# SSD decay with one additive mask and a per-head Exp on ScalarE, and the gated norm weight folded into w_out

## The chip, the cores and the metric

The kernel runs on one core of a Trainium2 chip. Its engines are TensorE (PE; its weight loads are listed apart as PEld), VectorE (DVE), ScalarE (ACT) and GpSimd (POOL); SyncE (SP) issues nearly all of the DMAs. The metric is the device time of one execution in microseconds (us), as the median of the runs; lower is better. Each engine works through its own instructions in order, and semaphores hold an instruction until what it needs is there.

## The reference, cut to what matters

The model is one step of a decoder trunk with two layers: a Mamba-2 SSD layer, then a latent attention layer (MLA), for a prompt of 1024 tokens and 8 samples of 8 tokens. The change lies wholly in the SSD layer. Its scan works in chunks of 128 tokens, with 32 heads of width 64 in 8 groups of 4 heads, and a state of 128 per head:

```
a = dt * a_head                          # a_head < 0, so a < 0
a_cs = cumsum(a)                         # within the chunk
decay[l, s] = exp(a_cs[l] - a_cs[s])     # for s <= l, else 0
y_diag = ((C B^T) * decay) @ (x * dt)    # per head, C B^T per group
states = B^T @ (x * dt * exp(a_cs[-1] - a_cs))
y_off  = (C @ state before the chunk) * exp(a_cs)
y = (y_diag + y_off + d_skip * x) * silu(z)
y = rms_norm over each group of 256 columns (y) * norm_w
out = y @ w_out
```

`norm_w` has one weight for each of the 2048 columns of y, and these columns are the rows of `w_out`, so `(y * norm_w) @ w_out` and `y @ (norm_w[:, None] * w_out)` are the same sum.

## The kernel before

**Matrix products.** Most of them are made in three passes over a high and a low part of each operand (`split`, lines 127 to 130: ScalarE copies the high part into a rounded type, VectorE or GpSimd subtracts it for the low part). The small products of the scan with the decay (lines 581 to 583) are made in full fp32.

**Stages.** `layer_ssd` (753) normalises x, projects group 0, works out dt and the cumulative sums for all tokens (`ssd_dt`, 335), and then runs over the groups: `ssd_scan` of group g gives a fraction of a step after each of its nine token tiles (eight prompt chunks and the 64 sample tokens), and the projections, convolution and gates of group g + 1 (`Group.steps`, 483) are traced in between. The scan of the last group is interleaved with the first half of the output projection (`ssd_outproj` "a", which needs groups 0 to 3 only: rows 0 to 1023 of `w_out`). The second half ("b") follows, and then the MLA layer.

**One tile of the scan, prompt case** (521 to 672). TensorE transposes x (two blocks) and B into one PSUM bank `trp` (537 to 540). ScalarE copies x out as `xsT` (542) and B as high and low parts. VectorE multiplies x by dt into `xdt` (555), from that PSUM bank. GpSimd multiplies `xsT` by tok slot 2 into `xdd` (558), which is split into `xddh` (ScalarE) and `xddl` (GpSimd); TensorE multiplies these with B into the state update `st` (586). TensorE makes the scores C B^T in the bank `cb`, of which there is one (569), and VectorE multiplies them by a 0/1 mask into `cbm` (571). A DMA on SP's queue copies the four heads' cumulative sums, spread over all partitions, into `M` (573; two buffers). Four VectorE instructions, one for each head, subtract the token's own sum and clip at zero (575); one ScalarE Exp covers all four heads (577); one VectorE product applies `cbm` (578); four matmuls multiply M by `xdt` into the bank `py` (582). Then y is put together by VectorE and GpSimd (656 to 661), ScalarE squares it and sums the squares (662), GpSimd multiplies it by the norm weight `nw` (663), and SP's queue stores it to `y_d` (664). The sample tile does the same with 64 tokens and also updates eight states; its product `pv` (603) uses the `cb` bank as well.

**Output projection.** `load_wout` (695) loads eight blocks of 128 rows of `w_out` for each half into two raw buffers, copies the high part on ScalarE (703) and subtracts the low part on GpSimd for even blocks and on VectorE for odd ones (704). A raw buffer is free for the next load when its low part is made. `ssd_outproj` (708) loads y, scales it by the group norms, transposes and splits it, and accumulates all eight blocks of a half into a bank `pj`, of which there are two (`poa` for the first half, `pob` for the second).

**What sets the order.** In the SSD layer nobody writes the order of an engine's instructions: the framework takes them by priority, which is program order, and places each at the time at which its own timing model thinks it ready. Buffers of a tag are handed out in turn. In the heads and the sample part of the MLA layer the order of TensorE and GpSimd is that of the program.

Of the kernel before, what the change touches and what calls it, by code (L numbers as in the profile page):

```python
# [36 lines left out]
NPG = PAST // PAGE  # L37
SCALE = (NOPE + ROPE) ** -0.5
NEG = -1e30
GB = 4  # L40
NKT = 4
LEAD = 2
# [101 lines left out]
def ssd_tiles(k):  # L144
    cp, nc = k.cs, k.nc
    k.masku = cp.tile([128, 128], F32, name="masku")
    k.masks = cp.tile([64, 128], F32, name="masks")
    k.blkm = cp.tile([64, NB], F32, name="blkm")
    k.yssq = cp.tile([128, 9, G], F32, name="yssq")
    k.tok = cp.tile([128, 9, 4, H], F32, name="tok")  # L150
    k.decp = cp.tile([128, H, 8], F32, name="decp")
    k.decs = cp.tile([128, 16, 8], F32, name="decs")
    k.dtb = cp.tile([128, H], F32, name="dtb")
    k.dsk = cp.tile([128, H], F32, name="dsk")
    k.tok3 = cp.tile([96, 2, H], F32, name="tok3")
    k.blk3 = cp.tile([96, 4], F32, name="blk3")
    k.alog = cp.tile([128, H], F32, name="alog")
    nc.sync.dma_start(k.alog, k.I["ssd_a_log"][0].partition_broadcast(128))
    nc.scalar.activation(k.alog, k.alog, AF.Exp)
    k.convT = cp.tile([128, 32, 24], F32, name="convT")  # L160


def ssd_consts(k):
    nc, I = k.nc, k.I
    nc.sync.dma_start(k.masku, I["c_masku"])
    nc.sync.dma_start(k.masks, I["c_masks"])
    nc.sync.dma_start(k.blkm, I["c_blkm"])
    for j in range(3):
        nc.sync.dma_start(k.blk3[32 * j : 32 * j + 32], I["c_blkm"][:32, :4])
    nc.gpsimd.memset(k.yssq, 1.0)  # L170
    nc.sync.dma_start(k.dtb, I["ssd_dt_bias"][0].partition_broadcast(128))
    nc.sync.dma_start(k.dsk, I["ssd_d"][0].partition_broadcast(128))
# [162 lines left out]
def ssd_dt(k, pool, psum):  # L335
    nc, I = k.nc, k.I
    blks = pool.tile([64, 128], F32, name="blks")
    nc.sync.dma_start(blks, I["c_blks"])
    ones = pool.tile([128, 128], F32, name="ones")
    nc.gpsimd.memset(ones, 1.0)  # L340
    alog = k.alog
    x = k.dtr.rearrange("p i h -> p (i h)")
    n = 9 * H
    u = pool.tile([128, n], F32, name="dtu")
    nc.scalar.activation(u, x, AF.Abs)
    nc.scalar.activation(u, u, AF.Exp, scale=-1.0)
    nc.scalar.activation(u, u, AF.Ln, bias=ones[:, 0:1])
    dt = pool.tile([128, n], F32, name="dt")
    nc.vector.scalar_tensor_tensor(dt, x, 0.0, u, op0=ALU.max, op1=ALU.add)
    a = pool.tile([128, 9, H], F32, name="dta")  # L350
    nc.vector.scalar_tensor_tensor(a, dt.rearrange("p (i h) -> p i h", h=H), -1.0,
                                   alog.unsqueeze(1).to_broadcast([128, 9, H]), op0=ALU.mult, op1=ALU.mult)
    af = a.rearrange("p i h -> p (i h)")
    pa = psum.tile([128, 512], F32, tag="y", name="dpa", bufs=PB["y"])
    pt = psum.tile([128, 512], F32, tag="y", name="dpt", bufs=PB["y"])
    for p, l, ls in ((pa, k.masku, k.masks), (pt, ones, blks)):
        nc.tensor.matmul(p[:, 0:256], l, af[:, 0:256], start=True, stop=True)
        nc.tensor.matmul(p[:, 256:288], ls, af[:64, 256:288], start=True, stop=True)
    acs = pool.tile([128, n], F32, name="acs")
    nc.vector.tensor_copy(acs, pa[:, :n])  # L360

    def tokv(j):
        return k.tok[:, :, j]

    def v(t):
        return t[:, :n].rearrange("p (i h) -> p i h", h=H)

    nc.gpsimd.tensor_copy(tokv(0), v(acs))
    nc.gpsimd.tensor_copy(tokv(1), v(dt))
    nc.vector.tensor_tensor(u, pt[:, :n], acs, op=ALU.subtract)  # L370
    nc.scalar.activation(u, u, AF.Exp)
    nc.vector.tensor_tensor(tokv(2), v(u), v(dt), op=ALU.mult)
    nc.scalar.activation(tokv(3), v(acs), AF.Exp)
    for j in range(3):
        for q in range(2):
            nc.sync.dma_start(k.tok3[32 * j : 32 * j + 32, q], k.tok[32 * q : 32 * q + 32, 8, 2])
    nc.scalar.activation(k.decp, pt[:, :256].rearrange("p (i h) -> p h i", h=H), AF.Exp)
    p = psum.tile([128, 512], F32, tag="tr", name="acsp", bufs=PB["tr"])
    for j in range(2):
        nc.tensor.transpose(p[:, j * 128 : j * 128 + 128], acs[:, j * 128 : j * 128 + 128], k.ident)  # L380
    nc.tensor.transpose(p[:H, 256:320], acs[:64, 256:288], k.ident[:64, :64])
    acsT = pool.tile([128, 320], F32, name="acsT")
    nc.vector.tensor_copy(acsT[:, :256], p[:, :256])
    nc.vector.tensor_copy(acsT[:H, 256:], p[:H, 256:320])
    k.acs_d = k.dram.tile([8, H, 128], F32, name="acs_d")
    k.acss_d = k.dram.tile([H, 64], F32, name="acss_d")
    nc.sync.dma_start(k.acs_d.rearrange("(j i) h t -> (i h) j t", j=2), acsT[:, :256].rearrange("p (j t) -> p j t", j=2))
    nc.sync.dma_start(k.acss_d, acsT[:H, 256:])
    sel = pool.tile([64, 2, 128], F32, name="selp")
    nc.gpsimd.memset(sel, 0.0)  # L390
    nc.gpsimd.memset(sel[:, 0, 0:64], 1.0)
    nc.gpsimd.memset(sel[:, 1, 64:128], 1.0)
    ra = pool.tile([64, 2, 16, NB], F32, name="ra")
    nc.vector.tensor_tensor(ra, a[:64, 8].rearrange("p (c two) -> p two c", two=2).unsqueeze(3)
                            .to_broadcast([64, 2, 16, NB]),
                            bass_bcast2(k.blkm, 2, 16), op=ALU.mult)
    pd = psum.tile([128, 512], F32, tag="tr", name="decp", bufs=PB["tr"])
    mm3(nc, pd[:, :128], [(sel[:, j], ra[:, j].rearrange("p c b -> p (c b)")) for j in range(2)])
    nc.scalar.activation(k.decs, pd[:, :128].rearrange("p (c b) -> p c b", b=NB), AF.Exp)
# [121 lines left out]
def ssd_scan(k, gr, pools):  # L521
# [2 lines left out]
    g = gr.g  # L524
    S = None
    hs = slice(4 * g, 4 * g + 4)
    nw = sp.tile([128, 256], F32, tag="nw", name=f"nw{g}", bufs=1)
    nc.sync.dma_start(nw, I["ssd_norm_w"][0, 256 * g : 256 * g + 256].partition_broadcast(128))
    for i in ORDER[g]:
        t0, m = TILES[i]  # L530
        sl = slice(t0, t0 + m)
# [19 lines left out]
        def v3(t):  # L551
            return t[:m].rearrange("p (h q) -> p h q", q=64)

        xdt = sp.tile([128, 256], F32, tag="xdt", name="xdt" + tag, bufs=2)
        nc.vector.tensor_tensor(v3(xdt), v3(p[:, 0:256]), hb(1), op=ALU.mult)  # L555
        if not smp:
            xdd = sp.tile([128, 256], F32, tag="xdd", name="xdd" + tag, bufs=1)
            nc.gpsimd.tensor_tensor(v3(xdd), v3(xsT), hb(2), op=ALU.mult)
# [8 lines left out]
        nc.gpsimd.tensor_tensor(v3(xD), v3(xsT), k.dsk[:m, hs].unsqueeze(2).to_broadcast([m, 4, 64]), op=ALU.mult)  # L567
        pc = psum.tile([128, 512], F32, tag="cb", name="cb" + tag, bufs=PB["cb"])
        nc.tensor.matmul(pc[:m, :m], B, C, start=True, stop=True)
        cbm = sp.tile([128, 128], F32, tag="cbm", name="cbm" + tag, bufs=1)  # L570
        nc.vector.tensor_tensor(cbm[:m, :m], pc[:m, :m], (k.masks if smp else k.masku)[:m, :m], op=ALU.mult)
        M = sp.tile([128, 4, 128], F32, tag="M", name="M" + tag, bufs=2)
        nc.sync.dma_start(M[:m, :, :m], (k.acss_d[hs] if smp else k.acs_d[i, hs]).partition_broadcast(m))
        for h in range(4):
            nc.vector.tensor_scalar(M[:m, h, :m], M[:m, h, :m], tk[:, 0, 4 * g + h : 4 * g + h + 1], 0.0,  # L575
                                    op0=ALU.subtract, op1=ALU.min)
        nc.scalar.activation(M[:m, :, :m], M[:m, :, :m], AF.Exp)  # L577
        nc.vector.tensor_tensor(M[:m, :, :m], M[:m, :, :m],
                                cbm[:m, :m].unsqueeze(1).to_broadcast([m, 4, m]), op=ALU.mult)
        py = psum.tile([128, 512], F32, tag="y", name="py" + tag, bufs=PB["y"])  # L580
        for h in range(4):
            nc.tensor.matmul(py[:m, h * 64 : h * 64 + 64], M[:m, h, :m], xdt[:m, h * 64 : h * 64 + 64],  # L582
                             start=True, stop=True)
        if not smp:
            ps = psum.tile([128, 512], F32, tag="st", name="st" + tag, bufs=PB["st"])
# [74 lines left out]
            nc.vector.tensor_tensor(y, py[:, :256], xD, op=ALU.add)  # L660
        nc.vector.tensor_tensor(y[:m], y[:m], z, op=ALU.mult)
        nc.scalar.activation(xD[:m], y[:m], AF.Square, accum_out=k.yssq[:m, i, g : g + 1])  # L662
        nc.gpsimd.tensor_tensor(y[:m], y[:m], nw[:m], op=ALU.mult)  # L663
        nc.sync.dma_start(k.y_d[sl, 256 * g : 256 * g + 256], y[:m])
        if i == 7:
            pf = psum.tile([128, 512], F32, tag="tr", name="pf" + tag, bufs=PB["tr"])
# [28 lines left out]
def load_wout(k, pool, raws, kks, ws):  # L695
    nc = k.nc
    wo = k.I["ssd_w_out"][0]
    for kk in kks:
        hi = pool.tile([128, D], F32R, name=f"woh{kk}")
        lo = pool.tile([128, D], F32R, name=f"wol{kk}")  # L700
        raw = load_raw(raws, 1, D)[:, 0]
        nc.sync.dma_start(raw, wo[kk * 128 : kk * 128 + 128])
        nc.scalar.copy(hi, raw)
        (nc.vector if kk % 2 else nc.gpsimd).tensor_tensor(lo, raw, hi.bitcast(F32), op=ALU.subtract)
        ws.append((hi, lo))


# [1185 lines left out]
```

## Time and profile before

| | |
|---|---|
| time, median of 3 runs | 2104.4 us (2102.95 to 2106.95) |
| span of the profiled execution | 2095.4 us |
| mean granted TensorE clock over the span | 0.969 |
| group 0's projections and dt | 0 to about 135 us |
| scans of groups 0 to 6 with the next group's projections | about 135 to 830 us |
| scan of group 7 with the first half of the output projection | about 850 to 1013 us |
| second half of the output projection | about 1013 to 1120 us |
| MLA layer | the rest |

The span runs from the first to the last instruction; 9.0 us of the median lie around it. A row of a window gives, for each engine, the time in which it was busy and in brackets the number of instructions, then the granted TensorE clock, the DMA share and GB/s. A row of instructions gives source line, engine, operation, what it writes and reads, the shape, the count, then busy us, mean ns of one, and the idle time of the engine just before them. A row of waits gives the waiting engine and line, what ended the wait, us in total, times, and in most views the longest.

### The profile page before, as it was taken

Reading aid. Unit: us, or ns where it says so; the run is one execution under the profiler, and the core shown is the slowest. Engines: PE = TensorE matmul, PEld = TensorE weight load, DVE = VectorE, ACT = ScalarE, POOL = GpSimd, SP = SyncE. Lnnn points to the kernel's source line nnn. Section 1 sums busy time; section 2 is a strip of 40 time slices with the busy share of each in tenths; the row PEclk is TensorE's granted clock in tenths of the full one; section 3 lists DMA queues with packets and bytes.
Section 4 is the critical chain, followed back from the end, with each engine's and each line's share of the span. In section 5 each row is a group of like instructions: output and inputs, shape, how many; then the busy total and the mean of one; then the engine's idle time right before and its main releaser. Section 6 shows DMA issues by size and latency. Waiting matters only on the chain.

```text
span 2095.4 us, 33766 instructions
## 1 busy us (share of the span) xinstructions
PE 1948.3 (93%) x12001; PEld 1763.6 (84%) x12001; DVE 1340.1 (64%) x2838; ACT 1043.3 (50%) x2287; POOL 851.9 (41%) x1059
## 2 busy tenths in 40 slices
PE   6999999999999999789998999699999999889998
PEld 5898999899999998677787998698888888778887
DVE  4558676767676767865334314366787778776665
ACT  5455565556565656522114323234676667755552
POOL 0337564646664646744000001102343334765541
PEclk9999999999999999889999999899999989999999
DMA  4222324231324241635534342132111112464451
GB/s 144 56 59 64 111 66 115 56 114 57 105 66 115 56 115 46 208 122 192 183 124 133 124 152 63 52 108 68 48 55 52 43 37 61 133 197 131 142 152 40
DMA packets 187631, 207.61 MB, mean 99 GB/s; under 512 B 23260, under 2 KB 153064, under 8 KB 187080
## 3 DMA queue, kind: packets, MB, share of 16 engines
q1 hardware_dynamic: 182408, 185.67, 29.2%
q0 software_dynamic: 4976, 19.66, 3.0%
q8 instruction: 95, 1.56, 0.3%
q14 instruction: 72, 0.59, 0.1%
q10 hardware_dynamic: 80, 0.13, 0.0%
HBM read 152.10 MB, written 53.28 MB: 98 GB/s over the span
## 4 chain that ended last, share of the span: by engine, by line
PE 33%; DVE 9%; issue 4%; POOL 4%; DMA 3%; ACT 2%; SPq 0%; POOLq 0%; DVEq 0%; ACTq 0%
PE pq L100 5%; PE pob L100 5%; PE pj L88 4%; PE poa L100 2%; POOL kvl L1541 2%; PE pk L100 1%; PE p L100 1%; PE vp L88 1%; PE st L1246 1%; DVE tl L1260 1%; PE st L1248 1%; PE st L1247 1%; PE o L1277 1%; PE sc L1214 1%; PE kp L88 1%
## 5 line engine op out<-in xcount | busy, mean ns | idle before, releaser
L88 PE MATMUL pj<-xh,wih 128*128 128x384 f32 (+1 forms) x768 | 254.9, 336 | 10.9 <-ACT xh L235 6.6
L88 PE MATMUL pj<-xl,wih 128*128 128x384 f32 (+1 forms) x768 | 255.9, 333 | 0.0
L88 PE MATMUL pj<-xh,wil 128*128 128x384 f32 (+1 forms) x768 | 255.1, 332 | 0.0
L1260 POOL TENSOR_TENSOR tl<-P,th 128x384 fp32r<-128x384 f32 (+1 forms) x96 | 90.7, 945 | 181.0 <-ACT P L1258 138.5
L88 PEld LDWEIGHTS pj<-xh,wih 128*128 128x128 f32 x768 | 145.8, 191 | 12.5 <-ACT xh L235 7.5
L468 DVE SCALAR_TENSOR_TENSOR acc<-raw,vec,acc 128x1112 f32<-128x1112 f32 x96 | 147.0, 1535 | 11.9 <-ACT acc L465 11.1
L88 PEld LDWEIGHTS pj<-xh,wil 128*128 128x128 f32 x768 | 146.3, 190 | 0.6
L88 PEld LDWEIGHTS pj<-xl,wih 128*128 128x128 f32 x768 | 146.1, 190 | 0.5
L575 DVE TENSOR_SCALAR M<-M,tok 128x128 f32<-128x128 f32 (+1 forms) x288 | 116.6, 462 | 43.0 <-DMA M<-acs_d 35.7
L100 PE MATMUL pz<-wih,xh 128*128 128x256 f32 x504 | 143.0, 287 | 0.0
L100 PE MATMUL pz<-wil,xh 128*128 128x256 f32 (+1 forms) x504 | 142.8, 287 | 0.0
L1257 ACT ACTIVATE th<-st 128x512 fp32r<-128x512 f32 x192 | 94.1, 490 | 73.6 <-PE st L1253 54.7
L100 PE MATMUL pz<-wih,xl 128*128 128x256 f32 x448 | 128.1, 286 | 0.0
L130 DVE TENSOR_TENSOR wil<-wraw,wih 128x512 fp32r<-128x512 f32 x88 | 70.4, 802 | 65.7 <-ACT wih L129 63.1
L1541 POOL TENSOR_TENSOR kvl<-pgr,kvh 128x1024 fp32r<-128x1024 f32 x32 | 78.2, 2445 | 67.8 <-ACT kvh L1540 67.8
L100 PEld LDWEIGHTS pz<-wih,xh 128*128 128x128 f32 x504 | 96.0, 190 | 1.1
L577 ACT ACTIVATE M<-M 128x512 f32<-128x512 f32 (+1 forms) x72 | 43.8, 608 | 102.0 <-DVE M L575 101.7
L1258 ACT ACTIVATE P<-st 128x512 f32<-128x512 f32 x192 | 93.2, 486 | 0.0
L100 PEld LDWEIGHTS pz<-wil,xh 128*128 128x128 f32 (+1 forms) x504 | 92.9, 184 | 0.3
L663 POOL TENSOR_TENSOR y<-y,nw 128x256 f32<-128x256 f32 (+1 forms) x72 | 64.5, 896 | 70.2 <-ACT xD L662 69.7
L582 PEld LDWEIGHTS py<-xdt,M 128*128 128x128 f32 (+1 forms) x576 | 70.4, 192 | 19.8 <-DVE xdt L555 6.5
L100 PEld LDWEIGHTS pz<-wih,xl 128*128 128x128 f32 x448 | 85.4, 191 | 0.4
(819 smaller groups left out, 6461.6 us busy)
## 6 DMA issues: line engine op xcount, KB each, us to landing
wraw<-in_ssd_w_in SPq DMA_DIRECT2D x92, 256.0 KB
M<-acs_d SPq DMA_DIRECT2D x64, 256.0 KB
s<-in_state_ssm SPq DMA_DIRECT2D x32, 256.0 KB
y_d<-y SPq DMA_DIRECT2D x64, 128.0 KB
out_s_ssm<-s SPq DMA_DIRECT2D x32, 256.0 KB
wraw<-in_ssd_w_out SPq DMA_DIRECT2D x16, 512.0 KB
q_d<-qt SPq DMA_DIRECT2D x32, 192.0 KB
qp<-q_d SPq DMA_DIRECT2D x8, 768.0 KB
```

What stands on the lines that cost most here:

```text
L88: nc.tensor.matmul(out, a, b, start=(i == 0), stop=(i == n - 1))
L100: nc.tensor.matmul(o, a, b, start=(j == 0), stop=(j == len(ops) - 1))
L130: (eng or nc.vector).tensor_tensor(lo, src, hi.bitcast(F32), op=ALU.subtract)
L468: nc.vector.scalar_tensor_tensor(acc, raw[:, j : j + n], k.convw[j][:, blk : blk + 1], acc, op0=ALU.mult, op1=ALU.add)
L575: nc.vector.tensor_scalar(M[:m, h, :m], M[:m, h, :m], tk[:, 0, 4 * g + h : 4 * g + h + 1], 0.0, op0=ALU.subtract, op1=ALU.min)
L577: nc.scalar.activation(M[:m, :, :m], M[:m, :, :m], AF.Exp)
L582: nc.tensor.matmul(py[:m, h * 64 : h * 64 + 64], M[:m, h, :m], xdt[:m, h * 64 : h * 64 + 64], start=True, stop=True)
L663: nc.gpsimd.tensor_tensor(y[:m], y[:m], nw[:m], op=ALU.mult)
L1257: nc.scalar.activation(th[:, :n], ps[:, :n], AF.Exp, scale=SCALE)
L1258: nc.scalar.activation(P[:, :n], ps[:, :n], AF.Exp, scale=SCALE)
L1260: eng.tensor_tensor(tl[:, :n], P[:, :n], th[:, :n].bitcast(F32), op=ALU.subtract)
L1541: nc.gpsimd.tensor_tensor(rl, raw, rh.bitcast(F32), op=ALU.subtract)
```

## The change

Three things are edited, all in the SSD layer.

1. The decay. tok slot 0 now holds ln dt minus the cumulative sum (with dt kept at 1e-37 or more before the logarithm), in place of the sum itself; slot 1, which held dt, is no longer written. The masks are turned into additive ones (0 or -1e30) once, on GpSimd. In the scan one VectorE addition puts the mask on all four heads, four ScalarE Exps with the head's slot 0 as bias give exp(a_cs[l] - a_cs[s]) * dt[s] or 0, and the product with the scores reads them from PSUM. So `cbm` and `xdt` are gone, and the matmuls take `xsT`.
2. The norm weight. The product of y with `nw` and the load of `nw` are gone. In `load_wout` the high part is the Copy of the raw block times the column of weights (one for each row), and the low part is raw times weight minus high.
3. The low part is made on VectorE for all blocks.

```
+TINY = 1e-37
...
+    k.negu = cp.tile([128, 128], F32, name="negu")
+    k.negs = cp.tile([64, 128], F32, name="negs")
...
+    for neg, mask in ((k.negu, k.masku), (k.negs, k.masks)):
+        nc.gpsimd.tensor_scalar(neg, mask, -NEG, NEG, op0=ALU.mult, op1=ALU.add)
...
-    nc.gpsimd.tensor_copy(tokv(0), v(acs))
-    nc.gpsimd.tensor_copy(tokv(1), v(dt))
+    lnd = pool.tile([128, n], F32, name="lnd")
+    nc.vector.tensor_scalar(lnd, dt, TINY, None, op0=ALU.max)
+    nc.scalar.activation(lnd, lnd, AF.Ln)
+    nc.vector.tensor_tensor(tokv(0), v(lnd), v(acs), op=ALU.subtract)
...
-    nw = sp.tile([128, 256], F32, tag="nw", name=f"nw{g}", bufs=1)
-    nc.sync.dma_start(nw, I["ssd_norm_w"][0, 256 * g : 256 * g + 256].partition_broadcast(128))
...
-        xdt = sp.tile([128, 256], F32, tag="xdt", name="xdt" + tag, bufs=2)
-        nc.vector.tensor_tensor(v3(xdt), v3(p[:, 0:256]), hb(1), op=ALU.mult)
...
-        cbm = sp.tile([128, 128], F32, tag="cbm", name="cbm" + tag, bufs=1)
-        nc.vector.tensor_tensor(cbm[:m, :m], pc[:m, :m], (k.masks if smp else k.masku)[:m, :m], op=ALU.mult)
         M = sp.tile([128, 4, 128], F32, tag="M", name="M" + tag, bufs=2)
         nc.sync.dma_start(M[:m, :, :m], (k.acss_d[hs] if smp else k.acs_d[i, hs]).partition_broadcast(m))
+        nc.vector.tensor_tensor(M[:m, :, :m], M[:m, :, :m],
+                                (k.negs if smp else k.negu)[:m, :m].unsqueeze(1).to_broadcast([m, 4, m]), op=ALU.add)
         for h in range(4):
-            nc.vector.tensor_scalar(M[:m, h, :m], M[:m, h, :m], tk[:, 0, 4 * g + h : 4 * g + h + 1], 0.0,
-                                    op0=ALU.subtract, op1=ALU.min)
-        nc.scalar.activation(M[:m, :, :m], M[:m, :, :m], AF.Exp)
+            nc.scalar.activation(M[:m, h, :m], M[:m, h, :m], AF.Exp, bias=tk[:, 0, 4 * g + h : 4 * g + h + 1])
         nc.vector.tensor_tensor(M[:m, :, :m], M[:m, :, :m],
-                                cbm[:m, :m].unsqueeze(1).to_broadcast([m, 4, m]), op=ALU.mult)
+                                pc[:m, :m].unsqueeze(1).to_broadcast([m, 4, m]), op=ALU.mult)
...
-            nc.tensor.matmul(py[:m, h * 64 : h * 64 + 64], M[:m, h, :m], xdt[:m, h * 64 : h * 64 + 64],
+            nc.tensor.matmul(py[:m, h * 64 : h * 64 + 64], M[:m, h, :m], xsT[:m, h * 64 : h * 64 + 64],
...
-        nc.gpsimd.tensor_tensor(y[:m], y[:m], nw[:m], op=ALU.mult)
...
-        nc.scalar.copy(hi, raw)
-        (nc.vector if kk % 2 else nc.gpsimd).tensor_tensor(lo, raw, hi.bitcast(F32), op=ALU.subtract)
+        nw = k.ssdn[:, kk : kk + 1]
+        nc.scalar.activation(hi, raw, AF.Copy, scale=nw)
+        nc.vector.scalar_tensor_tensor(lo, raw, nw, hi.bitcast(F32), op0=ALU.mult, op1=ALU.subtract)
```

## The prediction

> **What bounds the kernel now.** I read the page's busy times first, then windows over the stages that the change touches.
>
> ```profile
> PE 1948.3 (93%) x12001; PEld 1763.6 (84%) x12001; DVE 1340.1 (64%) x2838; ACT 1043.3 (50%) x2287; POOL 851.9 (41%) x1059
> ```
>
> ```profile
> 135.00:830.00 695.00, 667.70 (x4798) 643.98 (x4797) 515.01 (x1017) 392.35 (x898) 422.19 (x624) 0.99 0.30 85
> ...
> 850.00:905.00 55.00, 42.30 (x208) 34.71 (x209) 52.86 (x89) 25.71 (x58) 43.87 (x46) 0.81 0.64 209
> 905.00:1013.00 108.00, 100.04 (x498) 80.65 (x497) 54.13 (x85) 25.55 (x54) 37.40 (x39) 0.95 0.46 154
> ```
>
> Over the span TensorE is the bound, but an average hides two kinds of stage. From 135 to 830 us (scans of groups 0 to 6 under the next group's projections) TensorE is busy for 667.7 of 695 us at a clock of 0.99: whatever VectorE saves there, at most 695 - 667.7 = 27.3 us can come back. From 850 to 905 us it is the other way round: VectorE is busy for 52.9 of 55 us, and TensorE does 42.3 us at a clock of 0.81, which is 34.3 us of full-speed work, so 20.7 us are lost. The change adds or removes no matmul. It can only win back idle or slowed TensorE time, and it can only lose by making TensorE wait.
>
> Who ends TensorE's waits from 135 to 830 us:
>
> ```profile
> PE st L88 <- ACT xddh L129: 10.6, 13, 1.8
> PE py L582 <- DVE xdt L555: 5.2, 6, 1.6
> PE py L88 <- POOL Sl L130: 3.3, 6, 0.9
> PE py L582 <- DVE M L578: 2.9, 12, 0.6
> PE st L88 <- POOL xddl L130: 2.7, 8, 0.4
> PE s0p L631 <- DMA s<-in_state_ssm: 1.4, 2, 1.1
> PE pv L640 <- ACT sh L129: 0.7, 1, 0.7
> ```
>
> These sum to 26.8 us, so nearly all of the idle time is named. VectorE's decay chain ends 8.1 us of it (xdt and M); the chain xsT, xdd, xddh, xddl ends 13.3 us, on ScalarE and GpSimd. From 850 to 905 us:
>
> ```profile
> ACT M L577 <- DVE M L575: 9.2, 5, 3.5
> ...
> PE cb L569 <- DVE cbm L571: 3.1, 2, 2.6
> PE poa L100 <- ACT woh L703: 2.9, 1, 2.9
> ...
> PE st L88 <- DVE S L594: 1.4, 1, 1.4
> ```
>
> All of these go back to VectorE, also the third: the weight copy woh stands on ScalarE behind the Exp of M, and that behind the subtractions. The timelines of VectorE and ScalarE show it:
>
> ```profile
> 864.41 3.88 DVE L704 TENSOR_TENSOR wol<-wraw,woh 128x1024 fp32r<-128x1024 f32 x1
> 868.22 2.43 DVE L575 TENSOR_SCALAR M<-M,tok 128x128 f32<-128x128 f32 x4
> ```
>
> ```profile
> 870.68 0.63 ACT L577 ACTIVATE M<-M 128x512 f32<-128x512 f32 x1 [1.31 <-DVE M L575]
> 871.22 0.35 ACT L542 COPY xsT<-trp 128x256 f32<-128x256 f32 x1
> 871.47 1.05 ACT L703 CAST woh<-wraw 128x1024 fp32r<-128x1024 f32 x1
> ```
>
> **The change part by part.** VectorE first, with the whole run's means and then those from 850 to 905 us.
>
> ```profile
> L575 DVE TENSOR_SCALAR M<-M,tok 128x128 f32<-128x128 f32 x256 | 104.8, 467 | 36.0 <-DMA M<-acs_d 35.7
> L578 DVE TENSOR_TENSOR M<-M,cbm 128x512 f32<-128x512 f32 x64 | 51.9, 810 | 14.3 <-ACT M L577 13.7
> ...
> L646 DVE TENSOR_TENSOR s<-s,sn 128x512 f32<-128x512 f32 x32 | 21.8, 681 | 7.2 <-POOL s L641 4.9 <-PE sn L644 2.2
> ```
>
> ```profile
> L575 DVE TENSOR_SCALAR M<-M,tok 128x128 f32<-128x128 f32 x22 | 14.5, 709 | 0.1
> L704 DVE TENSOR_TENSOR wol<-wraw,woh 128x1024 fp32r<-128x1024 f32 x4 | 8.3, 2069 | 0.0
> L578 DVE TENSOR_TENSOR M<-M,cbm 128x512 f32<-128x512 f32 x7 | 6.7, 964 | 0.1
> ...
> L555 DVE TENSOR_TENSOR xdt<-trp,tok 128x256 f32<-128x256 f32 x6 | 2.5, 410 | 0.0
> ...
> L571 DVE TENSOR_TENSOR cbm<-cb,masku 128x128 f32<-128x128 f32 x7 | 1.9, 275 | 0.0
> ```
>
> A prompt tile loses four subtractions, cbm, xdt and the old product: 4 x 0.467 + 0.275 + 0.410 + 0.810 = 3.36 us. It gains the mask addition, two SBUF inputs of 512 columns like L578 (0.81 us), and the product with the scores in PSUM, which I price by L646, the nearest 512-column operation with one PSUM input (0.68 us). Net -1.87 us a tile, some -16 us for each group.
>
> The two rows of 512 columns differ in how they are held up: L578 takes 0.96 us where GpSimd is busiest, L646 stays at 0.68 us. The Trainium skill, "SBUF — State Buffer", section "SBUF: two separate sides", says that a VectorE instruction with two SBUF inputs and a GpSimd instruction lock each other out. By that rule the new product never waits for GpSimd and the mask addition still does, which is the pricing above; with both products at L578's price the tile would save 1.74 us in place of 1.87.
>
> ScalarE:
>
> ```profile
> L577 ACT ACTIVATE M<-M 128x512 f32<-128x512 f32 x64 | 40.5, 632 | 87.6 <-DVE M L575 87.3
> ...
> L235 ACT ACTIVATE xh<-xtp,vec 128x384 fp32r<-128x384 f32 x16 | 8.9, 578 | 5.9 <-PE xtp L234 5.9
> ...
> L430 ACT ACTIVATE xs<-acc 128x128 f32<-128x128 f32 x16 | 5.0, 311 | 0.0
> ```
>
> ```profile
> L452 ACT COPY raw<-pj 128x384 f32<-128x384 f32 x64 | 30.2, 477 | 27.9 <-PE pj L88 19.0 <-DVE acc L468 8.5 <-DMA nw<-in_ssd_norm_w 0.3
> ```
>
> No Exp of 128 columns with a bias column exists. Without one, 128 columns take 0.311 us (L430); a column operand adds about 0.578 - 0.477 = 0.10 us (L235 against L452, the same 384 columns out of PSUM). So four take between 1.24 and 1.65 us in place of 0.63; I take 1.5 us, near the upper end, since the bias is certain: +0.9 us a tile, +63 us in all. ScalarE would be busy for about 450 of the 695 us. Against that, Exp no longer stands 87.6 us behind four subtractions but behind one addition.
>
> The Trainium skill, "ScalarE: Activation LUTs", section "What ACT_TABLE_LOAD costs", gives 280 ns + 0.833 ns a column with a pointer bias, with 93 ns of overlap; by that estimate four Exps take 1.55 us, and the sum stays. It speaks against the change, since the fixed part is now paid four times.
>
> GpSimd:
>
> ```profile
> L663 POOL TENSOR_TENSOR y<-y,nw 128x256 f32<-128x256 f32 x64 | 55.6, 869 | 69.1 <-ACT xD L662 68.7 <-DMA nw<-in_ssd_norm_w 0.2
> L704 POOL TENSOR_TENSOR wol<-wraw,woh 128x1024 fp32r<-128x1024 f32 x8 | 19.5, 2436 | 14.6 <-ACT woh L703 14.6
> ```
>
> It loses the norm product (0.87 us a tile, and the store of y no longer waits for it) and eight low parts; the eight loads of nw leave SP's queue.
>
> Now the stages, as TensorE time.
>
> *Step 1, groups 0 to 6 (27.3 us idle).* Of the 8.1 us that xdt and M end, I count 6 as gone: xsT is ready before xdt was, and M has fewer instructions ahead of it. GpSimd's relief brings some 2 us of xddl and Sl. Against that, the scores now stay in the only cb bank until M is ready, where cbm emptied it at once; the next tile's scores matmul can stand in TensorE's queue on that. I take +3 us. Net -5 us. Bounds: -16 us if 27.3 us go down by three fifths, and the rivals' prices upward.
>
> *Step 2, 850 to 905 us.* VectorE loses 14.5 + 6.7 + 2.5 + 1.9 = 25.6 us. It gains 5.5 mask additions (22 / 4) at 0.96 = 5.3 us, seven products at 0.68 = 4.8 us and four more low parts, between 1.2 us (the shortest row of L704 on VectorE was 1.207 us) and 2.07 us each, so 4.8 to 8.3 us. Net -7.2 to -10.7 us of an engine that is full. I take -8 us, near the contended end. Bounds: zero, if loading sets the pace, and the whole -20.7 us.
>
> *Step 3, the second weight load.* The chain of waits shows it:
>
> ```profile
> 975.07 6.14 POOL yrsb L204
> 981.21 2.38 POOL wol L704
> 983.61 4.22 DMA wraw<-in_ssd_w_out
> ```
>
> ```profile
> 985.00:1000.00 15.00, 12.68 (x53) 10.24 (x53) 7.13 (x8) 5.18 (x6) 4.78 (x2) 0.89 0.67 218
> ```
>
> A low part on GpSimd stands behind a 6.14 us power, and with it the next load, ScalarE's woh, and behind that a copy for TensorE. On VectorE it doesn't. TensorE did 12.68 x 0.89 = 11.3 us in these 15, so at most 3.7 us; I take -2.5 us (zero to -3.7).
>
> *Step 4, dt.* Two VectorE instructions and one Ln replace two GpSimd copies.
>
> ```profile
> 121.61 1.28 ACT L347 ACT_TABLE_LOAD   x1
> ...
> 123.96 1.28 ACT L373 ACT_TABLE_LOAD   x1
> ```
>
> The Ln set is in from 122.9 us and the Exp set follows. If the new Ln falls between, it costs no load; else two, 2.6 us. The first Exp of M ran only at 141 us and TensorE has projections meanwhile, so +0.5 us (zero to +2.6).
>
> Sum: -5 - 8 - 2.5 + 0.5 = -15 us. The span goes from 2095.4 to 2080.4 us; with the 9.0 us around it that lie between this span and the median of 2104.4 us, the time is **2089.4 us**.
>
> **The rivals.**
> *Slower: the cb bank.* If the model that places instructions thinks M ready earlier than it is, TensorE comes to the next scores matmul before the product has emptied the bank, and everything queued behind stands. The price by the present waits on xdt and M: (5.2 + 2.9) / 18 = 0.45 us each; at all 72 tiles 32 us, so -15 + 32 = +17 us, 2121 us. It decides from about half of the tiles on. For it: TensorE already waits at this bank from 850 to 905 us (3.1 us). Against it: py follows the same product and waits only 2.9 us in 12 cases now.
>
> *No change: ScalarE takes it back.* 0.9 us more a tile stand ahead of xddh; if those waits (13, 0.8 us each) double to 21 us and step 1's gain goes, -15 + 5 + 10.6 = +0.6 us, 2105 us. The skill's fixed cost for each activation (same section) is the rule behind this. Against it: 87.6 us of waiting at Exp shrink.
>
> *No gain at the seam.* If loads and not VectorE set the stretch from 850 us, step 2 gives nothing: 2097 us, still a gain.
>
> **How the numbers follow.** Forecast 0.50 and seam without gain 0.10, both faster; ScalarE 0.15, within 0.2%; the cb bank 0.25, slower. A measurement of this kernel can tell about 0.2% (4.2 us) from no change. The low end is the forecast with step 1 at -10 us and step 2 at -15 us, 2077 us, and I take 2075; the high end, 2121, takes in the cb rival. The likeliest case's own range is 2075 to 2099 us.
>
> **What would show it.** Right: VectorE's busy time falls by over 90 us, ScalarE's rises by about 65; waits on xdt are gone; the window after 850 us shows TensorE's clock above 0.81 and the first half of the projection ends some 8 us earlier against the start of that stage. Wrong: waits of the scores matmul (L569) on the product with the scores in most tiles (the bank), more waits on xddh (ScalarE), or the same length from 850 us on with VectorE no longer full.

## The result and the profile after

The changed kernel takes **2083.7 us** (median of four runs, 2082.0 to 2089.4), beside 2103.7 us for the kernel before: a ratio of 0.9917, 95% interval [0.9896, 0.9938], so 0.8% faster. The forecast was 2089.4 us. The profiled execution took 2084.4 us with a span of 2082.6 us. So 1.8 us lie around a span, not the 9.0 us that the prediction took over; the profiled execution of the kernel before, with its span of 2095.4 us, must have been one of the quicker ones. Spans differ by 12.8 us, medians by 20.

The page's first line after the change, to be held against the same line in the prediction:

```profile
PE 1936.8 (93%) x12001; PEld 1761.3 (85%) x12001; DVE 1247.5 (60%) x2488; ACT 1102.9 (53%) x2516; POOL 806.3 (39%) x979
```

VectorE lost 92.6 us, ScalarE gained 59.6, GpSimd lost 45.6. The same three windows after the change (us, then busy time and count of PE, PEld, DVE, ACT, POOL, then clock, DMA share, GB/s):

```profile
135.00:830.00 695.00, 669.25 (x4861) 653.79 (x4860) 434.32 (x708) 450.53 (x1109) 405.66 (x567) 0.99 0.30 84
...
850.00:905.00 55.00, 48.45 (x255) 40.07 (x256) 39.50 (x65) 28.40 (x76) 31.53 (x39) 0.96 0.62 198
905.00:1013.00 108.00, 101.08 (x511) 80.18 (x510) 55.69 (x82) 25.85 (x51) 21.42 (x23) 0.98 0.53 168
```

From 850 us on the picture is the forecast one: VectorE is no longer full (39.5 of 55 us, before 52.9), TensorE's clock is 0.96 (before 0.81). The changed kernel is some 7 us ahead by then; in a window laid 7 us earlier, from 843 to 898 us, the figures are 42.8 us and 0.94. In the groups' stretch VectorE is 81 us lighter, and TensorE's busy time in those 695 us has hardly moved. Who ends TensorE's waits there now (from 135 to 820 us: us in total, times, longest):

```profile
PE pj L89 <- ACT raw L459: 13.7, 6, 2.9
PE st L89 <- ACT xddh L130: 5.8, 6, 1.6
...
PE st L89 <- POOL xddl L131: 2.5, 6, 0.8
PE py L89 <- POOL Sl L131: 0.8, 1, 0.8
PE py L583 <- DVE M L579: 0.2, 1, 0.2
```

The waits on xdt are gone, those on M and xddh are smaller, and no scores matmul waits for its bank. But the first line is new: the next group's projection waits 13.7 us for ScalarE to empty its bank `pj`. ScalarE's timeline shows such a case:

```profile
780.59 1.28 ACT L436 ACT_TABLE_LOAD   x1
781.88 1.92 ACT L436 ACTIVATE acc<-acc 128x2048 f32<-128x2048 f32 x1
783.81 1.28 ACT L578 ACT_TABLE_LOAD   x1
785.11 1.28 ACT L578 ACTIVATE M<-M,tok 128x128 f32<-128x128 f32 x4
786.40 1.28 ACT L437 ACT_TABLE_LOAD   x1
...
788.31 0.46 ACT L459 COPY raw<-pj 128x384 f32<-128x384 f32 x1
```

```profile
788.82 0.44 PE L89 MATMUL pj<-xh,wih 128*128 128x384 f32 x1 [2.83 <-ACT raw L459]
```

The copy of 0.46 us stands behind an activation of 1.92 us, the four Exps, and three loads of the function table (`ACT_TABLE_LOAD` in the rows) of 1.28 us each. TensorE stands for 2.83 us.

The best ruler for what follows is the start of the last matmul of a stage: of the gates of group 7 (`pz`, the end of groups 0 to 6), and of the first and second half of the output projection (`poa`, `pob`). All in us of one profiled execution each (the lower rows belong to experiments below):

| kernel | last pz | last poa | pz to poa | last pob | span |
|---|---|---|---|---|---|
| before | 845.8 | 1015.4 | 169.6 | 1123.0 | 2095.4 |
| before, once more | 846.0 | 1016.5 | 170.5 | 1124.7 | 2099.3 |
| changed | 839.3 | 998.0 | 158.7 | 1106.0 | 2082.6 |
| decay part alone | 849.7 | 1013.1 | 163.4 | 1121.5 | 2101.8 |
| norm part alone | 821.6 | 984.2 | 162.6 | 1093.1 | 2061.3 |

The change gains 6.5 us in groups 0 to 6 and 10.9 us at the seam (from the last `pz` to the last `poa`), and has 17.0 us at the last `pob`. Of these 12.8 are left at the end, because the MLA layer, which the change doesn't touch, took 976.6 us in this execution and 972.4 in that of before (974.6 in the one once more).

### The profile page after: what moved, and what is told of

Read it like the earlier page. It is cut to its first block, busy times and chain, and to the rows that moved or that the text cites. A ratio compares the mean times of both kernels' runs of the same rounds, so it can differ in the third digit from the quotient of the medians.

```text
span 2082.6 us, 33479 instructions
## 1 busy us (share of the span) xinstructions
PE 1936.8 (93%) x12001; PEld 1761.3 (85%) x12001; DVE 1247.5 (60%) x2488; ACT 1102.9 (53%) x2516; POOL 806.3 (39%) x979
## 4 chain that ended last, share of the span: by engine, by line
PE 61%; DVE 12%; DMA 8%; ACT 7%; POOL 6%; issue 5%; SPq 1%; POOLq 0%; DVEq 0%; ACTq 0%
PE pj L89 17%; PE pz L101 7%; PE pq L101 5%; PE pob L101 5%; PE poa L101 3%; PE py L583 2%; DMA M<-acs_d 2%; PE p L101 2%; PE pk L101 1%; DVE tl L1261 1%; POOL kvl L1542 1%; POOL xdd L561 1%; PE vp L89 1%; PE kp L89 1%; PE st L1247 1%
## 5 line engine op out<-in xcount | busy, mean ns | idle before, releaser
L101 PE MATMUL pz<-wil,xh 128*128 128x256 f32 (+1 forms) x504 | 141.4, 286 | 0.0
L578 ACT ACTIVATE M<-M,tok 128x128 f32<-128x128 f32 (+1 forms) x288 | 91.1, 386 | 67.4 <-DVE M L575 66.9
L561 POOL TENSOR_TENSOR xdd<-xsT,tok 128x256 f32<-128x256 f32 x64 | 61.5, 962 | 63.1 <-ACT xsT L547 58.3
L1261 DVE TENSOR_TENSOR tl<-P,th 128x512 fp32r<-128x512 f32 x96 | 68.2, 710 | 20.2 <-ACT P L1259 19.5
L575 DVE TENSOR_TENSOR M<-M,negu 128x512 f32<-128x512 f32 x64 | 55.2, 864 | 36.1 <-DMA M<-acs_d 36.1
```

The costliest lines, as they stand in the source:

```text
L101: nc.tensor.matmul(o, a, b, start=(j == 0), stop=(j == len(ops) - 1))
L575: nc.vector.tensor_tensor(M[:m, :, :m], M[:m, :, :m], (k.negs if smp else k.negu)[:m, :m].unsqueeze(1).to_broadcast([m, 4, m]), op=ALU.add)
L578: nc.scalar.activation(M[:m, h, :m], M[:m, h, :m], AF.Exp, bias=tk[:, 0, 4 * g + h : 4 * g + h + 1])
L1261: eng.tensor_tensor(tl[:, :n], P[:, :n], th[:, :n].bitcast(F32), op=ALU.subtract)
```

## The experiments

Each ratio is to the kernel before on the same chip, with its 95% interval; the runs of the kernel before had medians of 2096.6 to 2098.6 us there. The letters of the theories are those of each expectation; A and B of the first four runs are not those of the next.

### The two parts alone

Theory A gave most of the gain to the decay part, as the prediction's first two steps did; the rival B gave it to the other edits.

The decay part alone keeps the old product with `nw` and the old split of `w_out`:

```
...
+        nc.gpsimd.tensor_tensor(y[:m], y[:m], nw[:m], op=ALU.mult)
...
-        nw = k.ssdn[:, kk : kk + 1]
-        nc.scalar.activation(hi, raw, AF.Copy, scale=nw)
-        nc.vector.scalar_tensor_tensor(lo, raw, nw, hi.bitcast(F32), op0=ALU.mult, op1=ALU.subtract)
+        nc.scalar.copy(hi, raw)
+        (nc.vector if kk % 2 else nc.gpsimd).tensor_tensor(lo, raw, hi.bitcast(F32), op=ALU.subtract)
```

> Only the decay part: additive mask, four Exps, scores from PSUM, xsT in the matmuls; the norm product on GpSimd and the old weight split stay. Theory A (VectorE's load on the decay is what the stretch after the last group projection waited for): most of the gain is here, 12 to 16 us of the 20, and the first half of the output projection ends 6 us or more earlier after the last gate matmul than before (169.6 us there). Theory B (the weight load of the output projection set that stretch, through low parts that are late on GpSimd): only the gain of groups 0 to 6, 5 to 8 us, and the stretch stays within 2 us of 169.6 us.

Measured: 2101.9 us, ratio 1.0005 [0.9982, 1.0027]. Alone, the decay part is worth nothing. In the profiled execution it shortens the seam by 6.2 us and lengthens groups 0 to 6 by 3.9. Neither theory fits: the shorter seam is theory A's, but the gain of 12 to 16 us isn't there.

The norm part alone is the reverse: the change without every line of the decay.

> Only the norm part: no product with the norm weight on GpSimd, w_out scaled as it is split, all low parts on VectorE; the old decay stays. Theory A: four more low parts on a VectorE that is full there cost 5 to 8 us, GpSimd's relief and the second weight load give 3 to 5 back, so within 4 us of the kernel before. Theory B: 9 to 13 us faster, and the stretch from the last gate matmul to the end of the first half of the projection falls from 169.6 us to 160 us or less.

Measured: **2062.8 us, ratio 0.9827 [0.9790, 0.9864]**. That is 36 us faster than the kernel before, and better than the whole change. Groups 0 to 6 end 24.2 us sooner, and the seam is 7.0 us shorter. TensorE's waits from 135 to 820 us are these, and nothing else above 0.7 us:

```profile
PE s0p L629 <- DMA s<-in_state_ssm: 5.9, 6, 1.4
PE st L88 <- ACT xddh L129: 5.2, 8, 1.2
PE pz L100 <- ACT raw L452: 1.7, 1, 1.7
```

So the decay costs some 20 us on top of the norm part, and the two parts don't add up. Neither theory had expected a time this low, and the seam of 162.6 us isn't the 160 us or less that theory B asked for.

### The low parts on VectorE alone, and the kernel before once more

```
-        (nc.vector if kk % 2 else nc.gpsimd).tensor_tensor(lo, raw, hi.bitcast(F32), op=ALU.subtract)
+        nc.vector.tensor_tensor(lo, raw, hi.bitcast(F32), op=ALU.subtract)
```

> The kernel before with one edit: all low parts of w_out on VectorE, nothing scaled, the norm product stays on GpSimd. It separates the move of the low parts from the rest of the norm part. Theory A: no faster than before, up to 5 us slower, since VectorE is full in the first weight load. Theory B: 7 us or more faster.

Measured: ratio 0.9993 [0.9973, 1.0013], and pz to poa takes 171.3 us. By itself the move gives nothing, as theory A had it.

> The kernel before, unchanged, as a measure of what two profiles and two timings of one program differ by. The medians should agree within 0.2% (4 us). The profile of before had a span 12.8 us longer than that of after while the timed medians differ by 20 us; if the MLA layer of one program varies by some 4 to 8 us from execution to execution, this second profile shows it.

Measured: ratio 0.9993 [0.9973, 1.0012]; this is what the comparison gives for no change.

### What in the decay costs the 20 us

Two theories went in: A, that `xsT` is now held until the py matmuls have read it; B, the four Exps with their table loads.

```
-        xsT = sp.tile([128, 256], F32, tag="xsT", name="xsT" + tag, bufs=2)
+        xsT = sp.tile([128, 256], F32, tag="xsT", name="xsT" + tag, bufs=3)
```

> The changed kernel with three xsT buffers in place of two. The norm part alone ran in 2062.7 us and the whole change in 2083.7, so on top of the norm part the decay costs about 20 us. Theory A: xsT is now held until the py matmuls have read it (before, they read xdt), so ScalarE's next xsT copy waits for PE (11.5 us, 6 waits in the groups' stretch) and the projection's raw copies stand behind it. With three buffers that wait goes: 2066 to 2075 us, and last pz 6 us or more ahead of 839.3 us. Theory B: the four Exps in a row and the 12 more table loads on ScalarE hold the raw copies up, whatever the buffers: 2080 to 2087 us, last pz within 3 us of 839.

Measured: 2077.8 us, ratio 0.9906 [0.9878, 0.9935], not to be told from the change with two buffers (0.9917). ScalarE's wait on the py matmul is gone and TensorE's on the `pj` bank has halved, yet only some 6 us of it showed in the profiled execution, and none for certain in the ratio. The last pz is at 832.6 us, 6.7 us earlier, as theory A had it; the time lies between the ranges of both theories. The seam of this kernel takes 164.1 us, 5.4 more than with two buffers, though the work in it is the same. TensorE's two longest entries now:

```profile
PE st L89 <- ACT xddh L130: 6.8, 6, 2.1
PE pj L89 <- ACT raw L459: 6.0, 3, 2.9
```

The norm part with only `xdt` taken away (one Exp as before, ln dt folded into the subtraction):

```
-            nc.vector.tensor_scalar(M[:m, h, :m], M[:m, h, :m], tk[:, 0, 4 * g + h : 4 * g + h + 1], 0.0,
+            nc.vector.tensor_scalar(M[:m, h, :m], M[:m, h, :m], tk[:, 0, 4 * g + h : 4 * g + h + 1], 30.0,
...
-            nc.tensor.matmul(py[:m, h * 64 : h * 64 + 64], M[:m, h, :m], xdt[:m, h * 64 : h * 64 + 64],
+            nc.tensor.matmul(py[:m, h * 64 : h * 64 + 64], M[:m, h, :m], xsT[:m, h * 64 : h * 64 + 64],
```

> The norm part, and of the decay only that xdt goes: tok holds the cumulative sum minus ln dt, VectorE subtracts it with a clip at 30 in place of 0, one Exp over four heads as before, cbm as before, and the py matmuls read xsT. Leaves out nothing of the sum. Theory A (xsT held longer): 2070 to 2080 us, with a wait of ScalarE's xsT copy on the py matmul in the trace. Theory B (four Exps): 2055 to 2064 us, as fast as the norm part alone (2062.7) or a little faster, since 44 us of xdt products leave VectorE.

Measured: 2094.9 us, ratio 0.9985 [0.9962, 1.0008]. Taking away one VectorE product a tile, and adding nothing to ScalarE, costs 33 us against the norm part alone: more than the whole decay part does. Theory B is out as the only cause. Theory A's time (2070 to 2080 us) is missed by 15 us or more; the wait that it named is there, but at 12.9 us it is too small for 33:

```profile
ACT xsT L543 <- PE py L581: 12.9, 6, 2.2
```

The norm part with the additive mask and the four Exps, `xdt` kept:

> The norm part, and of the decay the additive mask, the four Exps with a bias and the scores read from PSUM; xdt stays (no ln dt). Theory A: 2058 to 2066 us, as the norm part alone. Theory B: 2076 to 2086 us, with PE waits on the raw copies of the pj bank of 10 us or more between 135 and 820 us and ScalarE at about 440 us there (398 in the norm part alone).

Measured: 2072.8 us, ratio 0.9893 [0.9864, 0.9923], between both theories, and without any wait on the `pj` bank, which B asked for (TensorE's longest entry there is xddl from GpSimd, 11.1 us). Three subsets of the decay cost 14 us (four Exps), 33 us (no xdt) and 19 us (all of it). Prices that don't add are no prices of instructions.

### Is the norm part's gain the wait behind the Square?

In the kernel before GpSimd multiplies y in place, so it has to wait until ScalarE's Square has read y:

```profile
POOL y L663 <- ACT xD L662: 63.1, 38, 3.0
```

The experiment makes the product in another tile, with the same instructions on the same engines:

```
-        nc.scalar.activation(xD[:m], y[:m], AF.Square, accum_out=k.yssq[:m, i, g : g + 1])
-        nc.gpsimd.tensor_tensor(y[:m], y[:m], nw[:m], op=ALU.mult)
-        nc.sync.dma_start(k.y_d[sl, 256 * g : 256 * g + 256], y[:m])
+        nc.scalar.activation(xdt[:m], y[:m], AF.Square, accum_out=k.yssq[:m, i, g : g + 1])
+        nc.gpsimd.tensor_tensor(xD[:m], y[:m], nw[:m], op=ALU.mult)
+        nc.sync.dma_start(k.y_d[sl, 256 * g : 256 * g + 256], xD[:m])
```

> The kernel before, with GpSimd's product with the norm weight written into xD and stored from there, and the Square's unused squares written into xdt, which the py matmuls have read by then. The same instructions and DMAs on the same engines, but GpSimd no longer waits for ScalarE's Square (63 us in 38 waits in the groups' stretch of the kernel before). Theory C (the norm part's 36 us are this wait, and xdd, xddl and Sl queued behind it): 2066 to 2078 us beside 2098 to 2104 before. Theory D (they are GpSimd's load, 72 products of 0.87 us, or the second weight load and the layout that follows): 2094 to 2102 us, last pz within 4 us of 846.

Measured: 2116.8 us, ratio 1.0094 [1.0064, 1.0124]: a wait less, and 20 us slower. The wait moved to what makes y, and TensorE waits more on everything:

```profile
POOL xD L663 <- DVE y L661: 44.5, 51, 2.2
```

```profile
PE st L88 <- ACT xddh L129: 12.6, 13, 4.2
PE py L582 <- DVE M L578: 8.9, 5, 2.0
PE pj L88 <- ACT raw L452: 7.2, 6, 1.6
PE py L88 <- POOL Sl L130: 6.8, 4, 1.8
```

Theory C fell, and theory D's figures were missed too: the last pz is at 869.5 us, where D had 846. What all these kernels share is that the framework orders each engine's instructions anew, by its own timing model, for each edit.

### The same work in another order

TensorE's 11579 traced instructions are the same list in all these kernels; only their order differs. So one kernel's order can be put on another's work, with edges that set the issue order and are no semaphore waits. The four kernels differ from those above in the list of places `s` and in this:

```
+        mine = [i for i in insts if i.engine == getattr(nc, name).engine]
+        p = np.cumsum(np.frombuffer(zlib.decompress(base64.b85decode(s)), "<i2").astype(int))
...
+        for a, b in zip(p[:-1], p[1:]):
+            tc.add_manual_dep(mine[b], mine[a].name,
+                              mybir.DependencyInfo(mybir.DependencyClass.NoSync, mybir.DependencyReason.DATA),
+                              reason="order")
```

The other engines are still ordered by the framework, around the order that is held. The traces show that they largely follow. Up to 840 us the kernel before with TensorE in the norm part's order has about 98% of VectorE's and ScalarE's instructions in the norm part's sequence, and only about half in the sequence of the kernel before. So in the first of the two tables below an order is nearly that of all engines. The edges don't seem to have brought waits of their own: the traces list 2416 semaphore waits at that kernel's matmuls, 2454 at those of the kernel before and 2422 at those of the norm part.

> The changed kernel with three xsT buffers (own order: ratio 0.9906 to the kernel before), with TensorE's instructions held in the order that the framework gave the norm part alone (ratio 0.9827). TensorE's 11579 traced instructions are the same list in all these kernels; a list of offsets and edges that set the issue order alone hold them. The other engines are ordered by the framework. Theory O (the framework's new order of TensorE is what the decay costs): ratio 0.980 to 0.985, 2056 to 2068 us. Theory B (four Exps and the table loads on ScalarE cost it, in any order): 0.988 to 0.993, or slower, because the order was made for a ScalarE with 40 us less work.

> The norm part alone (old decay, own order: ratio 0.9827) with TensorE held in the order of the changed kernel with three xsT buffers. Theory O: ratio 0.988 to 0.993, as that kernel with its own order (0.9906). Theory B: 0.980 to 0.985, the norm part keeps its time whatever the order.

> The kernel before, with TensorE held in the order of the norm part alone. The products with the norm weight stay on GpSimd, behind ScalarE's Square. Theory O: 0.980 to 0.988, most of the norm part's gain without the norm part. Theory L (GpSimd's 72 products and their wait are the cost): 0.995 to 1.005, TensorE waits for xddl and Sl from GpSimd 20 us or more in the groups' stretch.

> The norm part alone with TensorE held in the order of the kernel before. Theory O: 0.994 to 1.000 (the second weight load alone gives 5 to 8 us). Theory L: 0.980 to 0.987, since GpSimd is as free as in the norm part with its own order.

Measured, with the four kernels in their own orders in the same tables (an own order is marked * and comes from the runs above, each beside the kernel before on its own chip):

| norm part | in the order of before | in the order of the norm part |
|---|---|---|
| without it (the kernel before) | 1.0000 * | 1.0022 [1.0001, 1.0044] |
| with it | 0.9950 [0.9929, 0.9970] | 0.9827 [0.9790, 0.9864] * |

| decay part, three xsT buffers, on top of the norm part | in the order of the norm part | in the order of both parts |
|---|---|---|
| without it | 0.9827 [0.9790, 0.9864] * | 1.0047 [1.0020, 1.0074] |
| with it | 0.9986 [0.9959, 1.0014] | 0.9906 [0.9878, 0.9935] * |

Taken one by one, the first of the four landed in theory B's range (slower), the third in L's range by its ratio, though TensorE waited 10.5 us for xddl and Sl and not 20 or more, the fourth in O's, and the second, at 1.0047, in none. Neither theory O (the order alone) nor B or L (the work alone) gives such tables. **Work and order count only together.** With TensorE held in the order of before, the norm part gives 0.5%, some 10 us. The other 26 us need the new order, and that order gives the kernel before nothing. (In its profiled execution groups 0 to 6 end 7.4 us sooner, and the seam takes 6.2 us longer.) For the decay even the sign turns: in the norm part's order it costs 1.6% (33 us), in its own order the old decay is the one that costs 1.4% (30 us).

The mismatches can be read. Along TensorE's list, py stands in the median 42 matmuls behind its scores in the norm part's order and 30 in the order of both parts (counted along the two lists, groups 0 to 6), presumably because the new decay needs no `cbm`, and one addition in place of four subtractions. Put the old decay into the shorter lead, and TensorE waits for M:

```profile
PE py L580 <- DVE M L576: 25.3, 20, 3.9
PE py L580 <- DVE xdt L553: 6.1, 4, 2.4
```

Put the new decay into the longer one, and TensorE waits at the scores bank, as the prediction's slower rival had it, in four places and not in most tiles, 6.1 of the 8.1 us in the first of them:

```profile
PE cb L572 <- DVE M L579: 8.1, 4, 6.1
```

What stays open: why the framework's order for the norm part fits so well and that for the norm part without `xdt` so badly. No run held the order of VectorE, ScalarE and GpSimd, so how much of each difference is theirs isn't known, nor is a price of the decay that is free of any order. No run held a kernel in its own order either. All four crossed kernels are slower than the same kernels in their own orders, and a cost of the holding itself would show in the same way; that the traces show no more waits speaks against it, but it isn't ruled out.

## Why the prediction was right in its number and not in its reasons

**The number.** A change of -15 us was forecast. The two profiled spans differ by -12.8 us, the medians by -20.0, and the ratio of 0.9917 gives -17.4. The span was forecast at 2080.4 us and measured at 2082.6; the 9.0 us put around it should have been about 2.

**Step 1, groups 0 to 6: -5 us forecast, -6.5 measured, and the step still failed.** It counted "6 as gone" for xdt and M on VectorE, and "some 2 us" for GpSimd's relief. The waits on xdt and M went as it said. But the decay part alone, which takes those on xdt away and leaves 2.9 us on M, ends these groups 3.9 us later; the norm part alone, which is GpSimd's relief, ends them 24.2 us sooner; both together land by chance where the forecast stood. The hidden premise was that the rest of the schedule stays put while a wait is taken out. The rows of the whole stretch, from 135 us to the last `pz`, show how little the list of waits tells. Before, changed, decay alone and norm alone:

```profile
135.00:845.80 710.80, 683.50 (x4935) 659.55 (x4934) 522.30 (x1036) 401.32 (x914) 428.24 (x630) 0.99 0.30 85
```

```profile
135.00:839.30 704.30, 678.55 (x4941) 662.95 (x4939) 438.20 (x715) 455.95 (x1122) 407.83 (x569) 0.99 0.30 85
```

```profile
135.00:849.70 714.70, 679.79 (x4929) 659.20 (x4928) 438.99 (x716) 454.08 (x1116) 457.42 (x630) 0.99 0.30 84
```

```profile
135.00:821.60 686.60, 671.47 (x4934) 656.47 (x4932) 506.21 (x1037) 400.02 (x912) 384.87 (x568) 1.00 0.31 87
```

The count of matmuls is the same but for missing records. Idle time (the length less PE's busy time) is 27.3, 25.8, 34.9 and 15.1 us, and the busy time itself goes from 683.5 to 671.5. So the bound "at most 27.3 us can come back" wasn't passed, but its reason doesn't hold, since busy time shrinks too: the norm part brought 12.2 us of idle time and 12.0 us of busy time. Half clock (last section) doesn't explain that: 5.1 us are lost to it before and 1.7 in the norm part alone, but the second execution of the kernel before lost none, was busy for 681.2 us and ended these groups at 846.0 us all the same. What the rest of the 12.0 us is isn't settled. VectorE has 84 us less to do in the changed kernel, and these groups end 6.5 us sooner: VectorE wasn't what set their pace.

**The scores bank, +3 us in step 1, and the slower rival (2121 us).** In its own order TensorE of the changed kernel has no wait at the bank at all: in all 63 tiles of groups 0 to 6 the next scores stand behind the py of the tile, where in 15 tiles of the kernel before they stand ahead of it. The framework's order took care of the bank. The bank is real, as 8.1 us of it in a foreign order show, but it didn't decide.

**Steps 2 and 3, the seam and the second weight load: -10.5 us forecast together, -10.9 measured.** What step 2 started from is borne out: VectorE was full after 850 us and isn't any more. The rows from the last `pz` to the last `poa`, before and changed, show where the 10.9 us are:

```profile
845.80:1015.40 169.60, 147.11 (x735) 118.71 (x734) 111.16 (x180) 54.13 (x119) 83.03 (x86) 0.91 0.52 173
```

```profile
839.30:998.00 158.70, 139.62 (x734) 112.31 (x733) 96.83 (x149) 59.00 (x140) 60.47 (x69) 0.97 0.58 184
```

At these clocks about 15 us are lost before and 5 after (0.09 x 169.6 and 0.03 x 158.7), so some 10 of the 10.9 us are clock, the slowed time that step 2 wanted to win back. But that a VectorE with time to spare is the cause isn't shown. With only the low parts moved it is busy for 47.2 of the 55 us from 850 us on, and the stretch takes 171.3 us; in the kernel before held in the norm part's order it is busy for 42.6 us of a window laid the same way behind its last `pz`, and the stretch takes 175.8 us. The changed kernel with a third xsT buffer takes 164.1 us, at a clock of 0.93. So the agreement of the sum with the measured 10.9 us is in part luck. The parts alone shorten the stretch by 6.2 us (decay) and 7.0 us (norm), together by less than their sum; why isn't shown. Step 3's own reason, a low part behind a GpSimd power, isn't borne out either: with all low parts on VectorE the stretch took 171.3 us and not less than 169.6. What that move is worth in the changed kernel no run shows.

**Step 4, dt: +0.5 us forecast.** The first Exp of M starts at 142.0 us, before at 141.4: +0.6 us, close to the price. What TensorE felt of it isn't separated.

**The prices of the operations** held up. Rows of the changed kernel, by form (count, then busy us and mean ns, then idle before):

```profile
L578 ACT ACTIVATE M<-M,tok 128x128 f32<-128x128 f32 x256 | 82.5, 392 | 59.3 <-DVE M L575 58.9
L575 DVE TENSOR_TENSOR M<-M,negu 128x512 f32<-128x512 f32 x64 | 55.2, 864 | 36.1 <-DMA M<-acs_d 36.1
L579 DVE TENSOR_TENSOR M<-M,cb 128x512 f32<-128x512 f32 x64 | 43.2, 676 | 4.5 <-ACT M L578 4.0 <-PE cb L572 0.5
L578 ACT ACT_TABLE_LOAD x27 | 34.6, 1283 | 0.4
L705 DVE SCALAR_TENSOR_TENSOR wol<-wraw,vec,woh 128x1024 fp32r<-128x1024 f32 x16 | 21.3, 1338 | 7.3 <-ACT woh L704 7.3
```

The mask addition was priced at 0.81 us (0.86), the product with PSUM scores at 0.68 (0.68), four Exps at 1.5 us. The timeline above has them in 1.28 us, because they overlap (4 x 0.392 would be 1.57). The Trainium skill, "ScalarE: Activation LUTs", section "What ACT_TABLE_LOAD costs", gives 280 ns + 0.833 ns a column for an activation with a pointer bias and an overlap of 93 ns: an estimate of 387 ns for one of 128 columns and of 1.27 us for four, where the prediction's 1.55 us had left the overlap out. The trace agrees (392 ns for one, 1.28 us for four). Of the two new VectorE instructions only the addition, which takes both inputs from SBUF, has long cases: up to 1.39 us, and the product with the scores at most 0.69 us, which fits how they were priced. What the prediction didn't count is that the number of table loads moves: 27 at this line, for 21 in the kernel before:

```profile
L577 ACT ACT_TABLE_LOAD x21 | 26.9, 1283 | 3.2 <-DMA M<-acs_d 2.9
```

The cutting of one Exp into four isn't the reason. The norm part with the four Exps has 22 loads at this line, and the kernel with the norm product in another tile, with one Exp a tile, has 27. The changed kernel itself has 24 with three xsT buffers, and 22 when TensorE is also held in the norm part's order. So the number goes with the order and not with the pieces.

**ScalarE takes it back (2105 us).** The rival named xddh, whose waits fell from 10.6 to 5.8 us. Its engine was right and its place wrong: TensorE's new wait on ScalarE is for the `raw` copy. The decay part alone, at a ratio of 1.0005, is what this rival foretold for the whole; whether ScalarE is its cause isn't shown, since the four Exps on top of the norm part cost 14 us and the missing `xdt`, with no Exp added, 33.

## What to carry to other kernels

Where a framework orders the instructions by its own model, an edit changes the order of everything, and an equal list of TensorE instructions can move by 2% between two orders: test the parts of a change one by one, keep the best subset (here the norm part alone, 1.7%), and don't read the value of a part from the whole. A table of waits tells who came last in one order, not what a lighter engine will bring, and a forecast from it can have the right size by chance, as here. To tell work from order, hold the order of one kernel on the work of the other.

## What the runs showed of the hardware

A short stall of TensorE can be followed by half clock, and then costs more than its length. Here is one in the kernel before, first the matmul that waits, then windows of 2 us around it:

```profile
582.81 0.38 PE L88 MATMUL st<-xddh,BTh 128*128 128x256 f32 x1 [1.42 <-ACT xddh L129]
```

```profile
580.00:582.00 2.00, 1.40 (x10) 1.13 (x8) 2.00 (x6) 0.17 (x1) 2.00 (x5) 1.00 0.23 70
582.00:584.00 2.00, 0.97 (x5) 0.71 (x5) 2.00 (x4) 1.98 (x3) 1.45 (x3) 1.00 0.03 4
584.00:586.00 2.00, 1.90 (x8) 1.90 (x9) 2.00 (x4) 1.99 (x3) 0.92 (x4) 0.60 0.00 0
586.00:588.00 2.00, 2.00 (x12) 2.00 (x11) 0.64 (x2) 1.46 (x5) 1.17 (x2) 0.55 0.00 0
588.00:590.00 2.00, 2.00 (x17) 1.99 (x16) 1.44 (x4) 1.67 (x6) 2.00 (x4) 1.00 0.43 116
```

After 1.42 us without a matmul the granted clock is 0.60 and 0.55 in the next two full windows: (0.40 + 0.45) x 2 = 1.7 us are lost once more, and TensorE counts as busy meanwhile. The same matmul waits just as long in the second execution of the kernel before, and the clock stays at 1.00:

```profile
582.52 0.39 PE L88 MATMUL st<-xddh,BTh 128*128 128x256 f32 x1 [1.40 <-ACT xddh L129]
```

```profile
584.00:586.00 2.00, 1.95 (x15) 1.69 (x15) 1.86 (x4) 2.00 (x3) 0.65 (x1) 1.00 0.00 0
586.00:588.00 2.00, 2.00 (x18) 2.00 (x17) 0.78 (x2) 2.00 (x8) 1.45 (x2) 1.00 0.00 0
```

In groups 0 to 6 windows of 0.5 us show the loss in two sizes only, 1.7 us and 3.4 us, that is half clock for 3.4 or 6.8 us. In these groups the norm part alone has one such stretch (1.7 us lost), the kernel before two (3.4 and 1.7 us) and none in its second execution, the changed kernel five (1.7 us each), and the norm part in the order of both parts five. So a gap of this length doesn't bring one each time, and that the gap is the cause is an inference from what precedes the slow stretches. In the norm part alone too one of 1.41 us (the transposes of `s0p` at 723.4 us) was followed by a clock of 1.00. The Trainium skill, "TensorE: Matmul & The Clock Gate", section "What's actually happening", has the clock at half "after ≥1 idle window (~3.4µs)". The length of the slow stretches agrees with that window; the idle time needed doesn't, since the clock fell after 1.42 us here, and the measurement decides. What else it takes isn't shown.
